# Seven block products for eight in the last feed-forward network of a two-layer trunk, with weight sums by accumulating DMAs

## The chip, the cores and the metric

The kernel runs on one core of one Trainium2 chip. The metric is the time of one execution on the device in microseconds (us), the median over several runs of the same program. The profile is one execution taken by the hardware profiler.

## The reference

256 tokens of width 1024 in float32 go through two layers. Layer 0 is a feed-forward network (FFN), a gMLP mixer and a second FFN; layer 1 is an FFN, a stick-breaking attention on a shared K and V, and a second FFN; a final RMSNorm follows. Each FFN adds half of its result to the residual stream. Its hidden width is 2816. What the change touches is the last FFN and the norm behind it:

```python
def swiglu(h, w_in, w_out):
    gu = h @ w_in                       # [256, 1024] @ [1024, 5632]
    gate, up = jnp.split(gu, 2, axis=-1)
    return (jax.nn.silu(gate) * up) @ w_out   # [256, 2816] @ [2816, 1024]
...
x = x + FFN_RES_SCALE * swiglu(rms_norm(x, ffn_norm[i, 1]), ffn_w_in[i, 1], ffn_w_out[i, 1])
...
return rms_norm(x, final_norm)
```

## The kernel before

All products run on TensorE in float32r. To keep float32 accuracy each operand is split into two float32r parts, high and low, and `mm3` makes three products (low by high, high by low, high by high) for each one of the mathematics. The weights are a stream of pieces of [128, 1024]. `Weights.run_to` loads a piece with a DMA on the SP queue into a buffer `raw`, ScalarE casts it into `whi` (line 81), VectorE subtracts into `wlo` (line 83). There are 7 raw buffers and 9 of each part. A scheduler sets the order of each engine's instructions when the program is built, from the order of the code and from what is ready by its own reckoning; on the chip every engine then runs its list strictly in that order, and an instruction that waits holds up all behind it.

The last FFN works on 11 pairs of 128 hidden features, 256 features in a pair (NPAIR). For pair j, `ffn_in` computes gate and up, each [256 features, 256 tokens], into two PSUM banks (`gd`, `ud`) with 96 products of 256 columns, from 4 pieces of weights. VectorE scales both by 1/rms (lines 449, 451), ScalarE applies silu (450), VectorE multiplies (452), and `split` makes the parts `hhd` and `hld` (153, 154). `out_add` multiplies them with two pieces of the second matrix, tokens on the output's partitions: per pair 2 feature halves by 2 token halves by 2 column halves, 8 block products of [128x128] by [128x512], 24 products of 512 columns on TensorE, summed over all pairs in four banks `yo`. The products into `yo` of pair j stand behind the gate and up of pair j+1, so a whole pair of products covers VectorE's and ScalarE's work on h.

The last three chunks are worked piece by piece, and each piece of the output is added to `xo` (the residual stream, transposed back by `back`), squared and summed on ScalarE, multiplied by the gain on POOL, scaled by 1/rms and stored. POOL's queue has no DMA in this stage before; the only ones issued from it in the whole kernel are four copies within SBUF behind the K and V (line 663).

Of the kernel before, what the change touches and what calls it, by code (L numbers as in the profile page):

```python
# [901 lines left out]
```

## Time and profile before

| what | value |
|---|---|
| median of 3 runs | 1019.25 us (1019.13 to 1019.6) |
| profiled execution, first to last instruction (span) | 1016.9 us |
| mean granted TensorE clock | 0.998 |
| busy: PE, VectorE (DVE), ScalarE (ACT), POOL | 98%, 64%, 49%, 8% of the span |
| bytes from HBM | 176.73 MB, 175 GB/s over the span |
| first product of the last network | at 820.08 us |
| last product of the program | starts at 1009.26 us |

The span leaves out what lies ahead of the first and behind the last instruction; no other time of the profiled execution is given. The median of the runs is 2.35 us above the span. PE is matmul, PEld its weight load. A matmul's duration overlaps the next one's, so the pace is read from the distance of the starts. A row of a group gives busy time and mean duration, then how long the engine idled just ahead of such instructions, and for whom.

### The profile page before, as it was taken

What the parts mean: (1) busy time and instruction counts of PE and PEld (TensorE: products, weight loads), DVE (VectorE), ACT (ScalarE), POOL (GpSimd) and SP (SyncE); (2) the same over time, 40 slices, a digit from 0 to 9 for tenths busy, and PEclk for the clock granted to TensorE, in tenths of its full rate; (3) what the DMA queues carried; (4) which work ended last, traced back from release to release, by engine and by line L of the source; (5) the groups of instructions that cost most, each with busy time, mean ns of one, the idle gap of its engine ahead of it and who ended that gap; (6) DMA issues with size and microseconds to landing.
All of it is one profiled execution on the core that took longest, in us unless ns stands there. A gap on an engine that the chain in (4) does not pass through costs nothing.

```text
span 1016.9 us, 19320 instructions
## 1 busy us (share of the span) xinstructions
PE 998.7 (98%) x8044; PEld 979.4 (96%) x8044; DVE 651.4 (64%) x852; ACT 499.6 (49%) x683; POOL 84.0 (8%) x122
## 2 busy tenths in 40 slices
PE   9999999999999999999999999999998899999997
PEld 8999999999999999999999999999998799999996
DVE  6865665676766774646569655564679975655553
ACT  7543434475544553434348444443476565444433
POOL 3000000010000300000003000000036420000002
PEclk9999999999999999999999999999999999999999
DMA  9965555656545365655564756555642436656511
GB/s 310 325 187 174 185 179 176 187 161 212 186 167 167 125 214 183 187 184 187 180 190 141 239 185 187 182 188 181 193 132 65 137 117 219 188 185 191 183 42 42
DMA packets 135208, 179.56 MB, mean 177 GB/s; under 512 B 5624, under 2 KB 119376, under 8 KB 135120
## 3 DMA queue, kind: packets, MB, share of 16 engines
q1 hardware_dynamic: 134768, 177.76, 54.9%
q8 instruction: 63, 1.03, 0.4%
q0 software_dynamic: 192, 0.52, 0.2%
q14 instruction: 25, 0.20, 0.1%
q10 hardware_dynamic: 160, 0.05, 0.0%
HBM read 176.73 MB, written 1.05 MB: 175 GB/s over the span
## 4 chain that ended last, share of the span: by engine, by line
PE 88%; DVE 6%; issue 2%; ACT 1%; DMA 1%; POOL 1%; SPq 0%; ACTq 0%; POOLq 0%; DVEq 0%
PE yo L148 2%; PE yo L150 2%; PE yo L149 2%; PE gb L148 2%; PE uc L149 2%; PE gc L148 2%; PE ub L149 2%; PE yb L148 2%; PE uc L150 2%; PE ub L150 2%; PE ub L148 2%; PE gb L150 2%; PE uc L148 2%; PE ud L150 2%; PE gc L150 2%
## 5 line engine op out<-in xcount | busy, mean ns | idle before, releaser
L81 ACT CAST whi<-raw 128x1024 fp32r<-128x1024 f32 (+1 forms) x333 | 342.3, 1044 | 403.3 <-issue 219.2
L83 DVE TENSOR_TENSOR wlo<-raw,whi 128x1024 fp32r<-128x1024 f32 (+1 forms) x333 | 400.9, 1221 | 203.2 <-ACT whi L81 202.4
L288 POOL TENSOR_TENSOR acc<-acc,sq 128x256 f32<-128x256 f32 x39 | 33.9, 870 | 566.9 <-ACT sq L287 564.9
L148 PE MATMUL ga<-xnh,wlo 128*128 128x256 f32 x176 | 50.7, 288 | 0.0
L148 PE MATMUL ya<-hha,wlo 128*128 128x256 f32 x176 | 50.0, 284 | 0.1
L148 PE MATMUL yc<-hhc,wlo 128*128 128x256 f32 x176 | 50.0, 284 | 0.1
L148 PE MATMUL yb<-hhb,wlo 128*128 128x256 f32 x176 | 50.0, 284 | 0.0
L148 PE MATMUL gd<-xnh,wlo 128*128 128x256 f32 x176 | 50.0, 284 | 0.0
L148 PE MATMUL gb<-xnh,wlo 128*128 128x256 f32 x176 | 49.9, 283 | 0.0
L148 PE MATMUL gc<-xnh,wlo 128*128 128x256 f32 x176 | 49.9, 283 | 0.0
L149 PE MATMUL ya<-hla,whi 128*128 128x256 f32 x176 | 49.8, 283 | 0.0
L149 PE MATMUL yb<-hlb,whi 128*128 128x256 f32 x176 | 49.8, 283 | 0.0
L149 PE MATMUL yc<-hlc,whi 128*128 128x256 f32 x176 | 49.7, 283 | 0.0
L150 PE MATMUL ud<-xnh,whi 128*128 128x256 f32 x176 | 49.7, 282 | 0.0
L150 PE MATMUL uc<-xnh,whi 128*128 128x256 f32 x176 | 49.6, 282 | 0.0
L149 PE MATMUL ub<-xnl,whi 128*128 128x256 f32 x176 | 49.6, 282 | 0.0
L149 PE MATMUL uc<-xnl,whi 128*128 128x256 f32 x176 | 49.6, 282 | 0.0
L150 PE MATMUL yb<-hhb,whi 128*128 128x256 f32 x176 | 49.6, 283 | 0.0
L148 PE MATMUL ua<-xnh,wlo 128*128 128x256 f32 x176 | 49.6, 282 | 0.0
L150 PE MATMUL ga<-xnh,whi 128*128 128x256 f32 x176 | 49.6, 282 | 0.0
L150 PE MATMUL ub<-xnh,whi 128*128 128x256 f32 x176 | 49.6, 282 | 0.0
L149 PE MATMUL gd<-xnl,whi 128*128 128x256 f32 x176 | 49.5, 281 | 0.0
(286 smaller groups left out, 3367.1 us busy)
## 6 DMA issues: line engine op xcount, KB each, us to landing
raw<-in_ffn_w_in_dram SPq DMA_DIRECT2D x176, 512.0 KB, 4.6
raw<-in_ffn_w_out_dram SPq DMA_DIRECT2D x88, 512.0 KB, 4.2
raw<-in_a_w_in_dram SPq DMA_DIRECT2D x32, 512.0 KB, 4.4
raw<-in_a_w_out_dram SPq DMA_DIRECT2D x16, 512.0 KB, 3.3
raw<-in_b_w_q_dram SPq DMA_DIRECT2D x8, 512.0 KB, 4.4
raw<-in_b_w_o_dram SPq DMA_DIRECT2D x8, 512.0 KB, 4.3
raw<-in_w_kv_dram SPq DMA_DIRECT2D x4, 512.0 KB, 4.2
xin<-in_x_dram SPq DMA_DIRECT2D x4, 256.0 KB, 4.5
```

The source lines that it names most:

```text
L81: ins = nc.scalar.copy(hi[:, cc], raw[:, cc])
L83: ins = nc.vector.tensor_sub(lo[:, cc], raw[:, cc], hi[:, cc].bitcast(F32))
L148: nc.tensor.matmul(o, al, bh, start=first, stop=False, skip_group_check=True)
L149: nc.tensor.matmul(o, ah, bl, start=False, stop=False, skip_group_check=True)
L150: nc.tensor.matmul(o, ah, bh, start=False, stop=last, skip_group_check=True)
L288: nc.gpsimd.tensor_add(acc, acc, s)
```

## The change

In the last FFN the second matrix is multiplied with seven block products per pair instead of eight. The hidden values of a pair form a 2x2 matrix of blocks A (token half by feature half), its weights a 2x2 matrix B (feature half by column half of 512). Four sums of A blocks (S1 to S4) and four sums of B blocks (R1 to R4) enter seven products, one PSUM bank each (`q1` to `q7`); the four output blocks are sums of these banks, formed once at the end on `xo`.

- **A.** `in_half(j, m)` computes gate and up of only 128 features into one bank `i{j}_{m}` (48 products), from the same 4 weight pieces for m = 0 and 1. The bank pool `pi` has one buffer (seven banks are taken by `q`). VectorE scales the whole bank into `gud` (line 905), ScalarE applies silu to half of it (906), VectorE multiplies into `fs` (907). With m = 1 come four additions and subtractions of [128, 128] (910 to 913), a cast of [128, 896] on ScalarE into `fsh` and a subtraction on VectorE into `fsl` (156).
- **B.** The class `Forms` takes the second matrix out of the stream of pieces. `load` brings three blocks of 512 columns into `fraw` (two buffers). `first` splits all three (`fh0`, `fl0`, 1536 wide) and issues an accumulating DMA from POOL that adds the fourth block to two of them. `second` splits these two sums (`fh1`, `fl1`) and issues two more accumulating DMAs, the second of which reads what the first wrote. `third` splits the last two sums (`fh2`, `fl2`). Products 1, 2, 3 need `fl0`, 5 and 7 need `fl1`, 6 and 4 need `fl2`.
- **Buffers.** The stream has 5 raw buffers and 7 of each part, for the whole kernel. In the last FFN all 4 pieces of a pair are held until `in_half(j, 1)` has used them.
- **Order on TensorE.** `in_half(j, 0)`; products 1, 2, 3, 5 of pair j-1; `in_half(j, 1)`; products 7, 6, 4 of pair j-1.

```diff
-RAW_AHEAD = 7
-SPLIT_AHEAD = 5
+RAW_AHEAD = 5
+SPLIT_AHEAD = 4
...
-    rawp = ctx.enter_context(tc.tile_pool(name="rawp", bufs=7))
-    hip = ctx.enter_context(tc.tile_pool(name="hip", bufs=9))
-    lop = ctx.enter_context(tc.tile_pool(name="lop", bufs=9))
+    rawp = ctx.enter_context(tc.tile_pool(name="rawp", bufs=5))
+    hip = ctx.enter_context(tc.tile_pool(name="hip", bufs=7))
+    lop = ctx.enter_context(tc.tile_pool(name="lop", bufs=7))
...
-    plan11 = plan_ffn(1, 1)
+    plan11 = [
+        [[W.add(cols(ffn_w_in[1, 1], c0 + 256 * j, kh)) for c0 in (0, DFF)] for kh in range(2)] for j in range(NPAIR)
+    ]
...
+    psum.close()
+    pools["g"] = ctx.enter_context(tc.tile_pool(name="pi", bufs=1, space=PSUM))
+    pools["y"] = ctx.enter_context(tc.tile_pool(name="pq", bufs=7, space=PSUM))
...
+        def load(self, j):
+            t = fm.tile([P, 3, 512], F32, tag="raw", name=f"fraw{j}")
+            for s, (m, n) in enumerate(((1, 1), (0, 0), (1, 0))):
+                nc.sync.dma_start(t[:, s, :], self.block(j, m, n))
...
+        def split(self, j, step, s0, s1):
...
+                bufs = 1 if step == 2 else 2
+                h = fm.tile([P, n, 512], F32R, tag=f"h{step}", bufs=bufs, name=f"fh{step}_{j}")
+                l = fm.tile([P, n, 512], F32R, tag=f"l{step}", bufs=bufs, name=f"fl{step}_{j}")
+            nc.scalar.copy(h, t[:, s0:s1, :])
+            nc.vector.tensor_sub(l, t[:, s0:s1, :], h.bitcast(F32))
...
+        def first(self, j):
...
+            p["B22"], p["B11"], p["B21"] = self.split(j, 0, 0, 3)
+            nc.gpsimd.dma_start(
+                self.raw[j][:, 0:2, :],
+                self.block(j, 0, 1).unsqueeze(1).broadcast_to([P, 2, 512]),
+                accum_op=ALU.add,
+            )
...
+        def second(self, j):
...
+            p["R3"], p["R1"] = self.split(j, 1, 0, 2)
...
+            nc.gpsimd.dma_start(t[:, 1, :], self.block(j, 1, 1), accum_op=ALU.add)
+            nc.gpsimd.dma_start(t[:, 2, :], t[:, 1, :], accum_op=ALU.add)
...
+        def third(self, j):
...
+            p["R2"], p["R4"] = self.split(j, 2, 1, 3)
...
+        gu = scratch(f"gud{j}_{m}")
+        nc.vector.tensor_mul(pair(gu), pair(bank), bc2(rb))
+        nc.scalar.activation(gu[:, :T], gu[:, :T], AF.Silu)
+        nc.vector.tensor_mul(fs[j][:, 2 * m : 2 * m + 2, :], pair(gu[:, :T]), pair(gu[:, T:]))
+        if m:
...
+            nc.vector.tensor_sub(f[:, 4, :], f[:, 2, :], f[:, 0, :])
+            nc.vector.tensor_add(f[:, 5, :], f[:, 4, :], f[:, 1, :])
+            nc.vector.tensor_sub(f[:, 6, :], f[:, 0, :], f[:, 1, :])
+            nc.vector.tensor_sub(f[:, 7, :], f[:, 3, :], f[:, 5, :])
...
+            split(h, l, f[:, 1:, :])
...
-    for j in range(NPAIR - 2):
-        h = hs.pop(j)
-        for m in range(2):
-            out_add(W.get(plan11["out", j][m], UNIT), chunk(h, m), j == 0 and m == 0, False, range(2))
-        hs[j + 2] = ffn_in("d", j + 2, plan11["in", j + 2])
+    for j in range(1, NPAIR):
+        in_half(j, 0, gbank(f"i{j}_0"))
+        forms.first(j)
+        forms.third(j - 1)
...
+        if j + 1 < NPAIR:
+            forms.load(j + 1)
+        out_add(j - 1, (1, 2, 3, 5))
+        in_half(j, 1, gbank(f"i{j}_1"))
+        forms.second(j)
+        if j + 1 < NPAIR:
+            out_add(j - 1, (7, 6, 4))
+    forms.third(NPAIR - 1)
```

At the end of the program products 7, 6 and 4 of pair 9 and all seven of pair 10 remain; `rest` issues them one by one, and the sums into `xo`, squares and scaling follow each.

**VectorE, last network, a pair in the middle, before.** The rows from the scaling of pair 4's gate and up to the parts of its h and the next weight split (a name's first number is the pair or piece, the last one a running number).

```order
L449 TENSOR_TENSOR gsd_4_10550<-gd_4_10428,rb_119 128x512
L451 TENSOR_TENSOR usd_4_10551<-ud_4_10429,rb_119 128x512
L83 TENSOR_TENSOR wlo299_10601<-raw299_10560,whi299_10600 128x1024
L452 TENSOR_TENSOR usd_4_10551<-usd_4_10551,gsd_4_10550 128x512
L83 TENSOR_TENSOR wlo300_10607<-raw300_10578,whi300_10606 128x1024
L154 TENSOR_TENSOR hld_4_10557<-usd_4_10551,hhd_4_10556 128x512
L83 TENSOR_TENSOR wlo301_10661<-raw301_10598,whi301_10660 128x1024
```

VectorE splits at will between the four steps of h; the products of pair 4 that need `hld_4` stand behind the 96 products of pair 5.

**VectorE, the same place now.** The rows from the scaling of pair 6's second half (`gud6_1`) to that of pair 7's first half (`gud7_0`).

```order
L905 TENSOR_TENSOR gud6_1_11008<-i6_1_10959,rb_119 128x512
L83 TENSOR_TENSOR wlo299_11045<-raw299_11036,whi299_11044 128x1024
L83 TENSOR_TENSOR wlo300_11075<-raw300_11042,whi300_11074 128x1024
L907 TENSOR_TENSOR fs6_10929<-gud6_1_11008 128x256
L844 TENSOR_TENSOR fl1_7_11200<-fraw7_10943,fh1_7_11199 128x1024
L910 TENSOR_TENSOR fs6_10929<-fs6_10929 128x128
L844 TENSOR_TENSOR fl2_6_11119<-fraw6_10764,fh2_6_11118 128x1024
L911 TENSOR_TENSOR fs6_10929<-fs6_10929 128x128
L913 TENSOR_TENSOR fs6_10929<-fs6_10929 128x128
L156 TENSOR_TENSOR fsl6_11017<-fs6_10929,fsh6_11016 128x896
L905 TENSOR_TENSOR gud7_0_11109<-i7_0_11035,rb_119 128x512
```

Between `gud6_1` and `fsl6`, for which products 1, 2, 3 and 5 of pair 6 wait, stand two splits of weight pieces, one split of pair 7's weight sums (`fl1_7`) and one of pair 6's (`fl2_6`).

**ScalarE, the same place now.** The rows between the cast of pair 5's and of pair 6's sums of h (`fsh`).

```order
L906 ACTIVATE gud6_0_10930<-gud6_0_10930 128x256
L843 CAST fh0_7_11113<-fraw7_10943 128x1536
L81 CAST whi297_10901<-raw297_10893 128x1024
L81 CAST whi298_11038<-raw298_10899 128x1024
L81 CAST whi299_11044<-raw299_11036 128x1024
L81 CAST whi300_11074<-raw300_11042 128x1024
L906 ACTIVATE gud6_1_11008<-gud6_1_11008 128x256
L843 CAST fh1_7_11199<-fraw7_10943 128x1024
L843 CAST fh2_6_11118<-fraw6_10764 128x1024
L155 CAST fsh6_11016<-fs6_10929 128x896
```

Four casts of weight pieces stand between the silu of pair 6's two halves; `whi297` to `whi300` take the buffers of the four pieces that `in_half(6, 0)` and `in_half(6, 1)` use, from piece 290 on.

**VectorE, the beginning of the last network now.** The rows of pairs 1 and 2.

```order
L844 TENSOR_TENSOR fl1_1_10126<-fraw1_9859,fh1_1_10125 128x1024
L905 TENSOR_TENSOR gud1_1_10113<-i1_1_10064,rb_119 128x512
L83 TENSOR_TENSOR wlo278_10144<-raw278_9997,whi278_10143 128x1024
L83 TENSOR_TENSOR wlo279_10150<-raw279_10141,whi279_10149 128x1024
L907 TENSOR_TENSOR fs1_10027<-gud1_1_10113 128x256
L83 TENSOR_TENSOR wlo280_10180<-raw280_10147,whi280_10179 128x1024
L910 TENSOR_TENSOR fs1_10027<-fs1_10027 128x128
L844 TENSOR_TENSOR fl0_2_10219<-fraw2_10048,fh0_2_10218 128x1536
L911 TENSOR_TENSOR fs1_10027<-fs1_10027 128x128
L844 TENSOR_TENSOR fl2_1_10224<-fraw1_9859,fh2_1_10223 128x1024
L913 TENSOR_TENSOR fs1_10027<-fs1_10027 128x128
L905 TENSOR_TENSOR gud2_0_10214<-i2_0_10140,rb_119 128x512
```

The sums of pair 1's h (`fs1`) and the scaling `gud2_0`, which frees the only bank for gate and up, stand behind `fl0_2` and `fl2_1`, the latter behind pair 1's three accumulating DMAs.

## Rows read from the trace of the kernel before

**Rows 1.** The page, part 1: busy time, share of the span, instructions.
```profile
PE 998.7 (98%) x8044; PEld 979.4 (96%) x8044; DVE 651.4 (64%) x852; ACT 499.6 (49%) x683; POOL 84.0 (8%) x122
```
**Rows 2.** Stretches: PE, PEld, DVE, ACT, POOL busy; granted clock, DMA share, GB/s.
```profile
745.00:820.00 75.00, 66.81 (x495) 61.82 (x495) 65.96 (x112) 48.38 (x94) 31.07 (x57) 1.00 0.37 119
863.31:880.15 16.84, 16.84 (x122) 15.86 (x121) 9.57 (x11) 7.15 (x9) 0.00 (x0) 1.00 0.59 188
```
**Rows 3.** TensorE in time order around two pairs' ends: start us, us, what.
```profile
863.19 0.28 PE L150 MATMUL ud<-xnh,whi 128*128 128x256 f32 x1
863.31 0.40 PE L148 MATMUL yo<-whi,hld 128*128 128x512 f32 x1
...
864.47 0.40 PE L150 MATMUL yo<-whi,hhd 128*128 128x512 f32 x1
...
880.15 0.40 PE L148 MATMUL yo<-whi,hld 128*128 128x512 f32 x1
```
**Rows 4.** Groups by shape, 840 to 1000 us: busy us, mean ns, idle before, releasers.
```profile
L83 DVE TENSOR_TENSOR wlo<-raw,whi 128x1024 fp32r<-128x1024 f32 x53 | 64.0, 1220 | 41.5 <-ACT whi L81 41.4
L449 DVE TENSOR_TENSOR gsd<-gd,rb 128x512 f32<-128x512 f32 x10 | 6.9, 692 | 30.2 <-PE gd L150 30.2
...
L81 ACT CAST whi<-raw 128x1024 fp32r<-128x1024 f32 x52 | 53.7, 1047 | 76.4 <-issue 43.1 <-PE gd L150 31.4 <-PE yo L150 1.7
L153 ACT CAST hhd<-usd 128x512 fp32r<-128x512 f32 x11 | 6.9, 623 | 5.6 <-DVE usd L452 5.6
```
**Rows 5.** Groups by shape over the whole span: smaller shapes on VectorE and ScalarE.
```profile
L154 DVE TENSOR_TENSOR a1l<-at,a1h 128x256 fp32r<-128x256 f32 x8 | 3.4, 423 | 0.2
...
L320 DVE TENSOR_SCALAR diag<-ident,rT 128x128 f32<-128x128 f32 x12 | 2.9, 284 | 0.3
...
L856 ACT ACTIVATE junk<-xo 128x256 f32<-128x256 f32 x4 | 1.6, 409 | 2.3 <-DVE xo L854 2.3
```
**Rows 6.** VectorE in time order, back to back in the last network.
```profile
931.59 1.23 DVE L83 TENSOR_TENSOR wlo<-raw,whi 128x1024 fp32r<-128x1024 f32 x1
932.73 0.69 DVE L452 TENSOR_TENSOR usd<-usd,gsd 128x512 f32<-128x512 f32 x1
933.34 1.22 DVE L83 TENSOR_TENSOR wlo<-raw,whi 128x1024 fp32r<-128x1024 f32 x1
```
**Rows 7.** ScalarE in time order: casts and what they waited for (in brackets).
```profile
941.40 2.00 ACT L81 CAST whi<-raw 128x1024 fp32r<-128x1024 f32 x2 [3.92 <-PE gd L150]
```
**Rows 8.** The end of the last network in time order.
```profile
997.96 0.28 PE L150 MATMUL ud<-xnh,whi 128*128 128x256 f32 x1
...
1000.46 0.69 DVE L154 TENSOR_TENSOR hld<-usd,hhd 128x512 fp32r<-128x512 f32 x1 [0.69 <-ACT hhd L153]
...
1009.26 0.28 PE L150 MATMUL yo<-whi,hhd 128*128 128x256 f32 x1
```
**Rows 9.** DMA issues: engine, count, KB each, median us from issue to landing.
```profile
raw<-in_ffn_w_in_dram SPq DMA_DIRECT2D x176, 512.0 KB, 4.6
...
xin<-in_x_dram SPq DMA_DIRECT2D x4, 256.0 KB, 4.5
out_dram<-xo SPq DMA_DIRECT2D x4, 256.0 KB, 2.0
...
kzh<-kzh POOLq DMA_DIRECT2D x2, 128.0 KB, 6.2
```
**Rows 10.** The stretch of the POOL queue's copies (columns of rows 2), and their issue.
```profile
554.00:558.00 4.00, 4.00 (x36) 4.00 (x35) 3.94 (x9) 3.20 (x7) 2.51 (x4) 1.00 1.05 347
...
L663 POOL DMA_DIRECT2D kzh<-kzh x2 | 1.4, 684 | 9.2 <-ACT kzh L153 9.2
```
**Rows 11.** The chain of waits in the attention: start us, us, what.
```profile
791.57 2.48 DVE wlo L83 x2
...
798.69 2.59 DVE wlo L83 x2
```
**Rows 12.** The start of the last network in time order, POOL and TensorE.
```profile
821.86 4.25 POOL L288 TENSOR_TENSOR acc<-acc,sq 128x256 f32<-128x256 f32 x5
...
826.81 0.50 PE L311 MATMUL pstf<-ones,acc 128*128 128x1 f32 x4
```

More of the change, by code (lines that the diff above doesn't have):

```diff
@@ L806, in back @@
             for hf in range(2):
-                bank = gbank(f"xb{tt}{hf}")
+                bank = ybank(f"xb{tt}{hf}")
                 for c in range(4):
@@ new lines, in trunk, with out_add @@
+    q = {}
+    def out_add(j, which, last=False, cc=slice(0, 512)):
+        for n in which:
+            a, b = PRODUCTS[n]
+            s = SLOT[a]
+            mm3(
+                q[n][:, cc],
+                tuple(t[:, s, :] for t in fs[j]),
+                tuple(t[:, cc] for t in forms.parts[j][b]),
+                j == 0,
+                last,
+            )
+    norm = Rms("f3")
+    forms.load(0)
+    in_half(0, 0, gbank("i0_0"), (norm.columns, norm.rows))
+    forms.first(0)
+    forms.load(1)
@@ new lines, in trunk @@
+    in_half(0, 1, ybank("i0_1"))
+    back()
+    forms.second(0)
+    for j in range(1, NPAIR):
+        in_half(j, 0, gbank(f"i{j}_0"))
+        forms.first(j)
+        forms.third(j - 1)
+        if j == 1:
+            q = {n: ybank(f"q{n}") for n in range(1, 8)}
+        if j + 1 < NPAIR:
[6 more added lines that the diff above has]
+    forms.third(NPAIR - 1)
@@ new lines, in at, with add, square @@
+    def at(tt, n):
+        return xo[:, tt, n * 512 : (n + 1) * 512]
+    def add(o, a, scale, b):
+        nc.vector.scalar_tensor_tensor(o, a, scale, b, ALU.mult, ALU.add)
+    ss = {tt: small.tile([P, 4], F32, tag="ss", name=f"ss{tt}") for tt in range(2)}
+    def square(tt, i, cc):
+        junk = scratch(f"junk{tt}{i}", cc.stop - cc.start)
+        o = xo[:, tt, cc]
+        nc.scalar.activation(junk, o, AF.Square, accum_out=ss[tt][:, i : i + 1])
+        nc.gpsimd.tensor_mul(o, o, gf[:, cc])
@@ L871, in trunk @@
-        for hf in range(2):
-            cc = slice(hf * 512, (hf + 1) * 512)
-            nc.sync.dma_start(out[tt * P : (tt + 1) * P, cc], xo[:, tt, cc])
+        nc.vector.reduce_sum(v, ss[tt][:, :n], axis=mybir.AxisListType.X)
+        nc.vector.tensor_scalar(v, v, 1.0 / D, RMS_EPS, ALU.mult, ALU.add)
+        nc.scalar.activation(root, v, AF.Sqrt)
+        newton(r[:, 0:1], root, v, r[:, 1:2])
+        nc.vector.tensor_scalar_mul(at(tt, 0), at(tt, 0), r[:, 0:1])
+        nc.scalar.mul(at(tt, 1), at(tt, 1), r[:, 0:1])
@@ new lines, in finish, with rest @@
+        for h in range(2):
+            nc.sync.dma_start(out[tt * P : (tt + 1) * P, h * 512 : (h + 1) * 512], at(tt, h))
+    def rest(n, cc=slice(0, 512)):
+        if n in (7, 6, 4):
+            out_add(NPAIR - 2, (n,), False, cc)
+        out_add(NPAIR - 1, (n,), True, cc)
+    t1 = scratch("t1")
+    t5 = scratch("t5")
+    t6 = scratch("t6")
+    t7 = scratch("t7")
+    rest(1)
+    nc.scalar.mul(t1, q[1], 0.5)
+    rest(6)
+    nc.vector.tensor_add(at(1, 0), at(1, 0), t1)
+    nc.vector.scalar_tensor_tensor(
+        t6, q[6], 0.5, t1, ALU.mult, ALU.subtract
+    )
@@ new lines, in trunk @@
+    rest(5)
+    nc.vector.tensor_add(at(1, 1), at(1, 1), t6)
+    nc.scalar.mul(t5, q[5], 0.5)
+    rest(2)
+    add(at(1, 0), q[2], 0.5, at(1, 0))
+    square(1, 0, slice(0, 512))
+    nc.vector.tensor_sub(at(1, 1), at(1, 1), t5)
+    rest(3)
+    add(at(1, 1), q[3], 0.5, at(1, 1))
+    square(1, 1, slice(512, 1024))
+    rest(7)
+    add(t7, q[7], 0.5, t6)
+    nc.vector.tensor_add(at(0, 1), at(0, 1), t7)
+    nc.vector.tensor_sub(at(0, 1), at(0, 1), t5)
+    square(0, 0, slice(512, 1024))
+    nc.vector.tensor_sub(at(0, 0), at(0, 0), t7)
@@ L876 @@
+    finish(1, 2)
+    for i in range(2):
+        cc = slice(i * 256, (i + 1) * 256)
+        rest(4, cc)
+        add(xo[:, 0, cc], q[4][:, cc], 0.5, xo[:, 0, cc])
+        square(0, 1 + i, cc)
+    finish(0, 3)
 _INS = ['x', 'ffn_norm', 'ffn_w_in', 'ffn_w_out', 'mix_norm', 'a_w_in', 'a_ln_g', 'a_ln_b', 'a_w_s',
```

122 lines of the change are left out of this document (69 added, 53 removed).

## The prediction

> **What bounds the kernel now.** I read the page first: TensorE is busy for 98% of the span, VectorE for 64%, ScalarE for 49% [rows 1]. Then the stretches: in the last network TensorE is busy in all 16.84 us of a pair, VectorE in 9.57 and ScalarE in 7.15; only the attention leaves TensorE idle, 8.2 of its 75 us, with VectorE busy in 66 [rows 2]. TensorE in time order gives its pace: products of 512 columns start 0.232 us apart (five steps from 863.31 to 864.47), a pair takes 16.84 (863.31 to 880.15) [rows 3]. It has 24 of these and 96 of 256 columns, which leaves (16.84 - 24 x 0.232) / 96 = 0.117 for one of the latter. So in the last network the time is the number of products, as long as VectorE and ScalarE deliver in time. The groups show how much air they have: VectorE waits 30.2 us for `gd` and 41.4 for casts, and ScalarE's casts wait for `gd` [rows 4], that is for a weight buffer that TensorE still reads [rows 7].
>
> **What is saved.** One block product of eight, three products of 512 columns per pair: 3 x 0.232 x 11 = **7.65 us**. A pair would take 16.84 - 0.70 = 16.14.
>
> **What VectorE gets.** Durations: 1024 wide 1.22 us, 512 wide 0.69 [rows 4]; 256 wide 0.42, and 0.29 for 128 wide from the nearest shape, a one-input row of 0.284 [rows 5]. Instructions that follow each other start 0.085 sooner than their duration (1.14 and 0.61) [rows 6]. 896 and 1536 wide lie on the line through 512 and 1024: 1.09 and 1.75. Before, a pair has 6 x 1.22 + 4 x 0.69, about 10 us. Now 4 x 1.22 for pieces, 1.75 + 2 x 1.22 for the weight sums, 2 x 0.69 + 2 x 0.42 + 4 x 0.29 + 1.09 for h: 13.5, less 15 x 0.085, or 12.2 of 16.14. That would fit as a sum. It does not fit in its place.
>
> **The list behind each bank.** Count from the end of the last product of gate and up of a pair's second half (pair 6, say). Before, nothing waits soon for h, since 96 products of the next pair come first. Now TensorE has only products 7, 6, 4 of the pair before (9 x 0.232 = 2.09) and the next half (48 x 0.117 = 5.63), and is at product 1 of pair 6 after 7.72 less the overlap of the last product, 0.28 - 0.12: **7.56 us**. Product 1 needs `fsl6`. VectorE's list up to there:
> - Weight splits 297 and 298 stand ahead of `gud6_1` and take buffers that are free only when the first 24 products of this half are done, 24 x 0.117 = 2.81 before its end. Cast 1.05 [rows 4], two subtractions 2.28, two hand-overs 0.1: VectorE is late by 0.6.
> - `gud6_1` 0.61, two splits 2.28, `fs6` 0.34, `fl1_7` 1.14, one sum 0.20, `fl2_6` 1.14, two sums 0.48.
> - The cast of 896 on ScalarE, 0.94 between 0.62 and 1.05 [rows 4], `fsl6` 1.09, hand-overs 0.15.
>
> Together 8.97: TensorE **waits 1.4 us per pair**, twice what it saves. The pair takes 16.14 + 1.4 = 17.5, against 16.84. Nothing on ScalarE ends later: its four casts and the silu fit beside. The bank for gate and up itself is free in time, 1.3 us after the end where TensorE comes back after 2.1. Four sums of [128, 128] more or less in the estimate of 0.29 move this by 0.2 us.
>
> **The accumulating DMAs.** No accumulating DMA is in the trace. Plain neighbours [rows 9]: 256 KB to HBM 2.0 us from issue to landing, 256 KB from HBM 4.5, 512 KB 4.6; the four 128 KB copies from the POOL queue took 6.2, but in a stretch where the DMA engines were busy all the time (share 1.05) [rows 10], where the last network has 0.59 [rows 2]. I take 4.5 for each of the three, the row with the same bytes at the usual load, and keep 2.0 and 6.2 as ends; a gain is excluded, as there was no such wait. POOL is otherwise idle here; each issue costs it 0.68 [rows 10], no more than it has. In the middle of the stage 4.5 is hidden. `fraw` is free after `fl2`, 6.4 after the end above; load 4.5, cast 1.47, `fl0` 1.75 bring the first accumulation to 14.3, and ScalarE reaches `fh1` at 19.9 (17.5 + 2.4): room for 5.6 us. Each us above costs one in every pair. On POOL's queue the third accumulation waits for the second and holds up the next pair's first, which is not due before 14.3, when the third has landed (2 x 4.5 after `fl1` at 5.0). On SP the load of `fraw` waits for `fl2` and holds up the loads of pieces behind it, which have 12 buffers, three pairs, of air.
>
> In pairs 1 and 2 it is not hidden. `gud2_0`, which frees the bank, stands behind `fl2_1`. That needs DMAs two and three of pair 1; these start after `fl1_1`, which stands behind `fl2_0`, which needs DMAs two and three of pair 0. Four in series: 4 x 4.55 = 18.2. Between them: cast 1.05, `fl2_0` 1.14, a split 1.14, `fl1_1` 1.22, cast 1.05, `fl2_1` 1.14, a sum 0.20, `gud2_0` 0.69, hand-overs 0.2: 26.0 us from the end of `fl1_0`. TensorE has 1.0 left of a half there and one pair, 17.2: it waits **8.8 us** in all. Pair 2 still feels it (its `fl0` follows the late `fraw`), by the same lists 2.7.
>
> The Trainium skill (DMA: Bandwidth & Descriptors, Anatomy of one DMA — SWDGE (gpsimd) path) gives about 2.0 us plus the bytes at 436 GB/s, which would be an estimate of 3.2 and 2.6 us here and would bring my sum to about 1027; the copies of rows 10 took 6.2 where that rule gives 2.3, so under load this trace does not agree.
>
> **The ends of the stage.** At the start the one-column products for 1/rms stand behind 35 products, not 48: at 826.8 - 13 x 0.117 = 825.3 the sum of squares, done at 826.1, is not there [rows 12]: 0.8, taken as 1.0 with the hand-over. At the end nothing of the list stands in the way, but h of pair 10 takes 0.69 + 0.41 + 0.42 + 0.77 + 0.94 + 1.09 + 0.2 = 4.5 us (before 2.9, from the end of the last `ud` product at 998.24 to that of `hld` at 1001.15 [rows 8]), and TensorE has only 6 x 0.232 + 3 x 0.117 = 1.74 of other products, where before it had all those of pair 9: it waits **2.9**. Pair 9 waits 0.6 more (its VectorE list is shorter). Behind the last product little changes: the same add, square, root and scaling in two pieces, 0.
>
> **Fewer buffers.** Before the last network TensorE's order is the same. VectorE's chain in the attention has wlo splits in it [rows 11]; with the shorter look-ahead nine instead of ten stand between the first scan and the last values: -1.1, with bounds 0 and -1.2. Elsewhere the stream runs far ahead: 7 pieces cover 7 x 24 x 0.117 = 19.7 us of products, a load and a split take 4.6 + 1.05 + 1.22 = 6.9 [rows 4, 9]. 0.
>
> **The sum.** -7.65 + 1.0 (start) + 8.8 (pairs 0 and 1) + 2.7 (pair 2) + 6 x 1.4 = 8.4 (pairs 3 to 8) + 0.6 + 2.9 (end) - 1.1 = +15.7. The profiled execution's 1016.9 us would become 1032.6; with the 2.35 us by which the median stands above the span, **1035 us**. With 2.0 us for each DMA only the lists are left: pairs 0 to 2 wait 4.1 instead of 11.5 and pair 9 not at all, 1027. With 6.2 pairs 1 and 2 wait 4 x 1.7 = 6.8 and half of that, 3.4, more, pair 0 some 1.5, the end some 4, and six pairs 6.2 - 5.6 = 0.6 each: 19 more, 1054.
>
> **The rivals.**
> - *The list fits, faster.* If VectorE were 1.4 us earlier at `fsl` in each pair (no lateness from splits 297 and 298, and the sums behind each other cheaper than 0.20), and the DMAs took at most 2.5 us, only the start (1.0), pair 0 (1.0) and the end (2.9) would stay: 1019.25 - 7.65 - 1.1 + 4.9 = **1015**. For it: in sum VectorE has 16.1 - 12.2 us of air. Against it: all the durations are rows and the lists are fixed. It decides at a wait of 0.3 us per pair. 12%.
> - *The DMAs are slow, the pairs run at their pace.* From 5.6 us on the first accumulation sets each pair, and the four in series cost 4 us per us: 1054 at 6.2, about 1067 at 7.5. For it: 6.2 us for a quarter of the bytes [rows 10], and an accumulation must also read what it adds to. Against it: the load at that time. 20%. The Trainium skill (SBUF — State Buffer, Who interferes with whom) would push this way, as it says that POOL cannot write a DMA's descriptors while VectorE runs in a two-port mode; the copies of rows 10 were issued in 0.68 us each with VectorE busy in 3.94 of 4 us, so this trace shows no such starving.
> - *A draw.* Waits equal the saving, at 0.3 us per pair and fast DMAs: 1019. 5%.
> - That the change does not do what it says is excluded by the lists: 21 products of 512 columns per pair.
>
> **How the numbers follow.** The forecast has 63%, its own range 1024 to 1050 (DMAs of 2.0 to 5.8 us, the list 0.3 shorter or longer per pair). The range of 8 in 10 goes from 1018 to 1058: it leaves out the fast rival and the upper third of the slow one. A difference of 0.2% is what a measurement here can tell from none. Faster by over 0.2%: 12%. Within: 5%. Slower: 83%.
>
> **What would show it.** The products of a pair, waits aside, take 16.14 us; TensorE waits for VectorE's `fsl` (line 156) about 1.4 us in each of eight pairs, and for `gud2_0` some 6 us around pair 2; VectorE's busy time in a pair is about 13 us; accumulating DMAs land after about 4.5 us; about 3 us idle before product 1 of pair 10. I am wrong if TensorE's waits in the last network stay below 7.65 us, or if `fsl` is done before TensorE comes to it.

## The result and the profile after

The changed kernel takes **1075.43 us** (median of 4 runs, 1074.15 to 1076.56) against 1019.23 before (median of 4): a ratio of 1.055, 95% interval 1.0535 to 1.0565. The forecast was 1035, its range ended at 1058. The profiled execution has a span of 1074.7 us (before 1016.9), so there are 57.8 us to account for.

The page of the changed kernel: its header, then part 1, which answers to [rows 1], and the granted clock in the 40 slices.

```profile
span 1074.7 us, 19465 instructions
...
PE 1006.7 (94%) x7999; PEld 981.8 (91%) x7999; DVE 692.8 (64%) x922; ACT 522.6 (49%) x703; POOL 118.7 (11%) x154
...
PEclk9999999999999999999999999999999988989897
```

TensorE has 45 records fewer and yet 8.0 us more of busy time. Busy time that rises while work falls points to slower work, and the last line says where: the granted clock is below full in five of the last eight slices, which lie in the last network. The groups of waits of TensorE (us in total, times, longest) say what it stood still for:

```profile
PE q L150 <- DVE fsl L156: 27.5, 10, 4.8
PE i L150 <- DVE gud L905: 8.5, 1, 8.5
PE pstx L315 <- POOL acc L292: 5.8, 1, 5.8
PE q L150 <- DVE xo L972: 4.6, 1, 4.6
...
PE pstf L315 <- POOL acc L292: 1.9, 2, 1.6
```

The first, second and last are where the prediction put them. Of the first, 4.2 us belong to pair 0; the other 23.3, in pairs 2 to 10, stand against 14.6 forecast (2.7 + 8.4 + 0.6 + 2.9). The third, at the start of the program, and the fourth, at its end, were in no part of it. TensorE in time order, product 1 of pairs 2 to 10 without pairs 6 and 8, which waited 1.69 and 1.10 us (start us, us; in brackets the idle time before it and what ended it):

```profile
899.32 0.79 PE L150 MATMUL q<-fh,fsl 128*128 128x512 f32 x1 [3.87 <-DVE fsl L156]
...
919.45 0.50 PE L150 MATMUL q<-fh,fsl 128*128 128x512 f32 x1 [0.93 <-DVE fsl L156]
...
940.72 0.79 PE L150 MATMUL q<-fh,fsl 128*128 128x512 f32 x1 [4.81 <-DVE fsl L156]
...
960.66 0.50 PE L150 MATMUL q<-fh,fsl 128*128 128x512 f32 x1 [0.93 <-DVE fsl L156]
...
999.93 0.79 PE L150 MATMUL q<-fh,fsl 128*128 128x512 f32 x1 [4.68 <-DVE fsl L156]
...
1038.17 0.54 PE L150 MATMUL q<-fh,fsl 128*128 128x512 f32 x1 [2.21 <-DVE fsl L156]
...
1053.28 0.80 PE L150 MATMUL q<-fh,fsl 128*128 128x512 f32 x1 [3.11 <-DVE fsl L156]
```

In the middle there are two kinds of wait: some 1 us, near the forecast list wait of 1.4, and 3.9 to 4.8; those of 2.21 and 3.11 are the end's. The second column shows what the waits do to the product behind: 0.50 us behind the short ones, 0.79 behind most of the long ones. Behind the wait of pair 2 all twelve products (1, 2, 3 and 5, three each) ran slowly:

```profile
899.91 0.63 PE L151 MATMUL q<-fl,fsh 128*128 128x512 f32 x1
...
904.18 0.63 PE L152 MATMUL q<-fh,fsh 128*128 128x512 f32 x1
```

These start 0.427 us apart ((904.18 - 899.91) / 10), where products of this shape went at 0.232 before [rows 3]. The windows around them (stretch, length; PE, PEld, DVE, ACT, POOL busy; granted clock, DMA share, GB/s) show the clock: half, 1.2 GHz, and full again at 906:

```profile
902.00:903.00 1.00, 1.00 (x4) 0.76 (x3) 0.00 (x0) 0.00 (x0) 0.00 (x0) 0.50 0.98 178
...
906.00:907.00 1.00, 1.00 (x11) 1.00 (x10) 0.83 (x1) 0.00 (x0) 0.00 (x0) 1.00 0.00 0
```

What the long waits come from stands in the DMA issues of the last network (KB each, median us from issue to landing); the last three rows are the accumulating ones, for which [rows 9] gave the bounds:

```profile
fraw<-in_ffn_w_out_dram SPq DMA_DIRECT2D x33, 256.0 KB, 4.5
fraw<-in_ffn_w_out_dram POOLq DMA_DIRECT2D x11, 512.0 KB, 6.2
fraw<-in_ffn_w_out_dram POOLq DMA_DIRECT2D x11, 256.0 KB, 3.8
fraw<-fraw POOLq DMA_DIRECT2D x11, 256.0 KB, 3.8
```

One of the first kind, followed through POOL, ScalarE and VectorE ahead of product 1 of pair 2 (the three fences are the time orders of these engines):

```profile
886.35 1.20 POOL L850 DMA_DIRECT2D fraw<-in_ffn_w_out_dram  x1 [0.83 <-DVE fl L844]
```
```profile
893.33 2.01 ACT L843 CAST fh<-fraw 128x1024 fp32r<-128x1024 f32 x2 [3.63 <-DMA fraw<-in_ffn_w_out_dram]
```
```profile
894.41 1.23 DVE L844 TENSOR_TENSOR fl<-fraw,fh 128x1024 fp32r<-128x1024 f32 x1 [2.67 <-ACT fh L843]
...
895.75 1.22 DVE L844 TENSOR_TENSOR fl<-fraw,fh 128x1024 fp32r<-128x1024 f32 x1
896.89 0.28 DVE L913 TENSOR_TENSOR fs<-fs 128x128 f32<-128x128 f32 x1
898.17 1.09 DVE L156 TENSOR_TENSOR fsl<-fs,fsh 128x896 fp32r<-128x896 f32 x1 [1.00 <-ACT fsh L155]
```

From the start of the issue to the cast that needs the sum 7.0 us pass. VectorE stands still for 2.67 us at `fl1`, and the last sums of h and `fsl`, which do not need these weights at all, stand behind it in its list. That is the slow-DMA rival at work.

The balance, by parts of the span (forecast from the prediction's sum; measured from starts of the same product in both traces and from TensorE's idle times; the products saved are not measured but counted, at the pace before):

| part | forecast | measured |
|---|---|---|
| program start | 0 | +7.9 |
| pace of the products ahead of the last network | 0 | -3.3 |
| attention | -1.1 | -1.2 |
| products saved (counted) | -7.65 | -7.65 |
| TensorE idle in the last network: start | 1.0 | 1.6 |
| pairs 0 and 1 | 8.8 | 12.7 |
| pair 2 | 2.7 | 3.9 |
| pairs 3 to 8 | 8.4 | 14.1 |
| pair 9 | 0.6 | 2.2 |
| ahead of products of pair 10 | 2.9 | 3.1 + 4.6 |
| products at the lower clock | 0 | +16.5 |
| behind the last product | 0 | +1.0 |
| not assigned | | +2.4 |

The 16.5 are 67 products of 512 columns that start 0.437 us apart on average instead of 0.229, and 23 of 256 at 0.231 instead of 0.118. This is a tally of slow products: time that TensorE would have waited for VectorE even at the full clock is in it too.

### The profile page after: what moved, and what is told of

Its sections match the earlier page's. It is cut to its first block, busy times and chain, and to the rows that moved or that the text cites. A ratio compares the mean times of both kernels' runs of the same rounds, so it can differ in the third digit from the quotient of the medians.

```text
span 1074.7 us, 19465 instructions
## 1 busy us (share of the span) xinstructions
PE 1006.7 (94%) x7999; PEld 981.8 (91%) x7999; DVE 692.8 (64%) x922; ACT 522.6 (49%) x703; POOL 118.7 (11%) x154
## 4 chain that ended last, share of the span: by engine, by line
PE 72%; DMA 9%; DVE 8%; ACT 4%; issue 3%; POOL 2%; SPq 0%; ACTq 0%; POOLq 0%; DVEq 0%
DMA fraw<-in_ffn_w_out_dram 6%; DVE fl L844 2%; PE uc L152 2%; PE uc L151 2%; PE gc L150 2%; PE ua L150 2%; PE gc L151 2%; PE uc L150 2%; PE gc L152 2%; PE ua L151 2%; PE yb L150 2%; PE ua L152 2%; PE yb L152 2%; PE yb L151 2%; PE gb L150 2%
## 5 line engine op out<-in xcount | busy, mean ns | idle before, releaser
L150 PE MATMUL i<-xnh,wlo 128*128 128x256 f32 x352 | 100.2, 285 | 8.5 <-DVE gud L905 8.5
L152 PE MATMUL i<-xnh,whi 128*128 128x256 f32 x352 | 99.7, 283 | 0.0
L151 PE MATMUL i<-xnl,whi 128*128 128x256 f32 x352 | 99.5, 283 | 0.0
L844 DVE TENSOR_TENSOR fl<-fraw,fh 128x1024 fp32r<-128x1024 f32 (+1 forms) x33 | 46.2, 1399 | 60.2 <-ACT fh L843 60.1
L150 PEld LDWEIGHTS i<-xnh,wlo 128*128 128x128 f32 x352 | 67.2, 191 | 9.7 <-DVE gud L905 8.7
L843 ACT CAST fh<-fraw 128x1024 fp32r<-128x1024 f32 (+1 forms) x33 | 38.6, 1190 | 64.4 <-DMA fraw<-in_ffn_w_out_dram 32.8
L151 PEld LDWEIGHTS i<-xnl,whi 128*128 128x128 f32 x352 | 67.2, 191 | 0.8
L152 PEld LDWEIGHTS i<-xnh,whi 128*128 128x128 f32 x352 | 67.1, 190 | 0.0
L151 PE MATMUL ua<-xnl,whi 128*128 128x256 f32 x176 | 50.4, 287 | 0.0
L152 PE MATMUL ua<-xnh,whi 128*128 128x256 f32 x176 | 50.4, 286 | 0.0
```

What stands on the lines that cost most here:

```text
L150: nc.tensor.matmul(o, al, bh, start=first, stop=False, skip_group_check=True)
L151: nc.tensor.matmul(o, ah, bl, start=False, stop=False, skip_group_check=True)
L152: nc.tensor.matmul(o, ah, bh, start=False, stop=last, skip_group_check=True)
L843: nc.scalar.copy(h, t[:, s0:s1, :])
L844: nc.vector.tensor_sub(l, t[:, s0:s1, :], h.bitcast(F32))
```

## The experiments

**The DMAs.** My theory after the result: the accumulating DMAs make the long waits, and the waits the low clock. First the kernel without accumulating DMAs, which leaves the sums of the weights out of the result.

```diff
-            nc.gpsimd.dma_start(
-                self.raw[j][:, 0:2, :],
...
-            t = self.raw[j]
-            nc.gpsimd.dma_start(t[:, 1, :], self.block(j, 1, 1), accum_op=ALU.add)
-            nc.gpsimd.dma_start(t[:, 2, :], t[:, 1, :], accum_op=ALU.add)
```

> The changed kernel without its three accumulating DMAs per pair; all splits stay, so the sums of the second matrix are left out of the computation (R1 to R4 are plain blocks). Theory 'the DMAs set the waits beyond the list': the wait at gud2_0 (8.5 us) goes, the waits for fsl fall to 1.0 to 1.4 us in each pair, the clock stays at 2.4 GHz in the pairs, only the end (3.1 and 4.6 us) remains: idle in the last network 42 -> about 20 us, low clock 17 -> about 6, so about 1042 us. Rival 'VectorE's list is that long by itself': waits for fsl stay at 0.9 to 4.8 us and the time over 1065 us.

Measured: 1038.01 us, ratio 1.0188 (1.0167 to 1.0208). Its waits for `fsl` (`gud` is down to 0.8 us):

```profile
PE q L150 <- DVE fsl L156: 10.9, 9, 3.1
```

Product 1 of two pairs in time order:

```profile
882.13 0.50 PE L150 MATMUL q<-fh,fsl 128*128 128x512 f32 x1 [0.92 <-DVE fsl L156]
899.47 0.50 PE L150 MATMUL q<-fh,fsl 128*128 128x512 f32 x1 [0.92 <-DVE fsl L156]
```

Without these DMAs only the list is left: seven waits of 0.92 us, a pair of 17.34. Products at the lower clock cost some 4.5 us instead of 16.5. The DMAs cost 37 us in all.

Is it the adding, or a DMA as such? The same DMAs that copy instead of adding:

```diff
-                accum_op=ALU.add,
...
-            nc.gpsimd.dma_start(t[:, 1, :], self.block(j, 1, 1), accum_op=ALU.add)
-            nc.gpsimd.dma_start(t[:, 2, :], t[:, 1, :], accum_op=ALU.add)
+            nc.gpsimd.dma_start(t[:, 1, :], self.block(j, 1, 1))
+            nc.gpsimd.dma_start(t[:, 2, :], t[:, 1, :])
```

> The changed kernel with the same three DMAs per pair as plain copies, with no addition (the sums are left out of the computation). Theory 'adding makes the DMA slow': the 512 KB one lands in about 4.5 us where it took 6.2 and the 256 KB ones in about 2.5 where they took 3.8; the waits shrink by about 2 us in every second pair and some 6 us around pair 2, with the clock about 1055 us. Rival 'the queue and the load make it slow, not the addition': 6.2 and 3.8 us stay, the time stays at 1072 to 1077 us.

Measured: 1051.25 us, ratio 1.0318 (1.0297 to 1.0338). The same three rows of its DMA issues:

```profile
fraw<-in_ffn_w_out_dram POOLq DMA_DIRECT2D x11, 512.0 KB, 4.3
fraw<-in_ffn_w_out_dram POOLq DMA_DIRECT2D x11, 256.0 KB, 3.9
fraw<-fraw POOLq DMA_DIRECT2D x11, 256.0 KB, 2.4
```

Adding costs 1.9 us on the first kind and 1.4 on the third, nothing on the second. These 3.3 us per pair are worth 24 us of the time (1075.43 - 1051.25), the copying DMAs that remain 13.

**The clock.** If the lower clock comes from TensorE standing still, useless products in the gaps must bring it back. Sixteen products of 512 columns ahead of product 1, from pair 1 to pair 9:

```diff
+        if j > 1:
+            for _ in range(FILL):
+                nc.tensor.matmul(
+                    q[1], xnh[:, 0, :P], forms.parts[j - 1]["B11"][0], start=False, stop=False, skip_group_check=True
+                )
```

> The changed kernel with 16 extra products of 512 columns ahead of product 1 of each pair from the second on (they are added into q1, so the output has them too much). They need nothing that VectorE makes late, so TensorE works where it waited for fsl. They are 9 x 16 x 0.23 = 33 us of products more. Theory 'the waits lower the clock, and the products behind a long wait pay for it': the waits for fsl behind products of pairs 2 to 10 (23 us) nearly vanish and the clock stays at 2.4 GHz there, 11 us won back: 1075.4 + 33 - 23 - 11 = 1074 us, granted clock above 0.98. Rival 'the clock falls for another reason (what VectorE, ScalarE or the DMAs do)': the stretches at half clock stay, 1085 us or more, granted clock 0.97 or less.

Measured: 1078.08 us, ratio 1.0581 (1.056 to 1.0602). The same stretch of the changed kernel and, second, of this one (columns as in the windows above):

```profile
890.00:910.00 20.00, 16.13 (x102) 14.77 (x101) 9.94 (x15) 6.83 (x7) 2.96 (x3) 0.83 0.75 197
```
```profile
890.00:910.00 20.00, 20.00 (x136) 18.40 (x135) 12.71 (x16) 9.15 (x11) 2.14 (x4) 1.00 0.77 201
```

Nine pairs have 9 x 16 x 0.23 = 33 us more of products, and the time rises by 2.7. What they replace is mostly waiting: TensorE's idle time in the last network falls from 42.2 to 20.8 us, and about half of the 16.5 at the lower clock goes. So the clock follows the gaps, as the theory said, and the rival's 1085 us did not come. From product 1 of pair 2 to that of pair 9 TensorE now works without a pause:

```profile
903.82:1043.17 139.35, 139.35 (x933) 128.16 (x931) 85.59 (x107) 60.76 (x66) 21.60 (x22) 1.00 0.63 164
```

That is 19.91 us for each of seven pairs, which is what TensorE's own products take (16.14 + 16 x 0.23 = 19.8); the changed kernel took 138.85 for the same seven (899.32 to 1038.17). So the DMAs and VectorE's lists keep up with a pair of 19.9 us, but here they do not set it, the useless products do. Fewer of them were not tried, and no run takes away the low clock alone: what it costs by itself stays open.

**The start.** The wait of 5.8 us at `pstx` was not in the prediction. The time orders of POOL at the start of the program, before and, second, after:

```profile
14.11 0.78 POOL L347 TENSOR_TENSOR sqx<-xT 128x256 f32<-128x256 f32 x1 [0.77 <-ACT xT L342]
...
17.43 1.68 POOL L288 TENSOR_TENSOR acc<-acc,sq 128x256 f32<-128x256 f32 x2
25.06 2.07 POOL L500 TENSOR_SCALAR_AFFINE_SELECT wsbs<-wsbs 128x512 f32<-128x512 f32 x2 [5.95 <-DMA wsbs<-in_a_w_s_dram]
```
```profile
17.07 1.23 POOL L504 TENSOR_SCALAR_AFFINE_SELECT wsbs<-wsbs 128x512 f32<-128x512 f32 x2 [3.58 <-DMA wsbs<-in_a_w_s_dram]
18.26 1.58 POOL L351 TENSOR_TENSOR sqx<-xT 128x256 f32<-128x256 f32 x1
...
23.94 1.52 POOL L292 TENSOR_TENSOR acc<-acc,sq 128x256 f32<-128x256 f32 x2
```

The selection on `wsbs`, for which nothing waits early, has moved ahead of the sum of squares, for which TensorE waits, and it waits for its own load first. Theory: the smaller numbers of buffers alone do that. The kernel before, with these alone:

```diff
-RAW_AHEAD = 7
-SPLIT_AHEAD = 5
+RAW_AHEAD = 5
+SPLIT_AHEAD = 4
...
-    rawp = ctx.enter_context(tc.tile_pool(name="rawp", bufs=7))
+    rawp = ctx.enter_context(tc.tile_pool(name="rawp", bufs=5))
```

(`hip` and `lop` likewise, 9 to 7.)

> The kernel before, with nothing but 5 raw buffers and 7 of each part (5 loads and 4 splits ahead). Theory 'POOL at the start': fewer loads ahead let the load of wsbs go out earlier, and with it POOL's selection of wsbs moves ahead of the sum of squares, so that pstx waits some 5.8 us and TensorE's clock falls behind it. The first ya product then comes 7.9 us later than before, and with the 3.3 us won back on the way and 1.2 in the attention the last network begins 3.4 us later: about 1022.7 us. Rival, my prediction's: fewer buffers cost nothing outside the attention and win 1.1 there: 1018.1 us, no wait at pstx.

Measured: 1025.86 us, ratio 1.0073 (1.0056 to 1.009). Its wait:

```profile
PE pstx L311 <- POOL acc L288: 6.0, 1, 6.0
```

The last network begins at 827.05 instead of 820.08. The selection stands ahead of the sum of squares on POOL here too (16.52 against 17.71 us). So "fewer buffers, 0" cost 7 us, by an order on POOL. The expected value was missed by the 3.3 us of pace that this kernel did not gain; where those come from is shown at the pools below. Then the changed kernel with the selection held in its written place:

```diff
-        nc.gpsimd.affine_select(
+        ins = nc.gpsimd.affine_select(
...
+        tc.keep_in_program_order(ins)
```

> The changed kernel with one line more: POOL's selection of wsbs keeps its place behind the sum of squares at the start. Theory 'POOL at the start': the wait at pstx (5.8 us) and the low clock behind it go, 7.9 us in all: 1067.5 us. Rival: the start is late because weight pieces come late with 5 raw buffers; then the wait only moves to the first products of ua and the time stays at 1073 to 1076 us.

Measured: 1072.36 us, ratio 1.0525 (1.0509 to 1.0541). The wait at `pstx` is gone and the last network begins at 816.99, 6.5 earlier, but only 3.1 arrive at the end, between the two values expected: the last network then took 245.25 us from first to last product instead of 242.52. TensorE's idle time in it is the same (42.5 us, before 42.2), only with long waits in other pairs; what grew, by some 2.5 us, is the time at the lower clock. Why a start at another moment changes that was not tried.

**The end.** The changed kernel issues product 4 of pair 10 in two halves, and the second half's bank waits 4.6 us for VectorE's `xo`. In one piece there is no such wait:

```diff
+    rest(4)
...
-        rest(4, cc)
```

> The changed kernel with one thing else at its end: product 4 of pairs 9 and 10 is made in one piece of 512 columns, so that it doesn't wait for VectorE to read the first half of q4. Theory 'VectorE's list sets the end': TensorE's wait of 4.6 us for xo goes, but the end gains 1.3 us only, since VectorE comes to q4 at 1064.8 either way: 1074.1 us. Rival 'the wait is on the path': 1070.8 us.

Measured: 1076.21 us, ratio 1.0554 (1.0539 to 1.0569): no difference. The wait is gone from its list of waits and the end stays, so it was off the path: VectorE's sums set the end. Without the wait 14.9 us lie behind TensorE's last product, where 7.7 lay in the kernel before. In them one row stands out, here of the changed kernel (VectorE, and POOL beside it):

```profile
1060.81 0.68 DVE L972 SCALAR_TENSOR_TENSOR t<-q,t 128x512 f32<-128x512 f32 x1
...
1061.81 1.78 DVE L1023 TENSOR_TENSOR xo<-xo,t 128x512 f32<-128x512 f32 x1
1063.52 0.68 DVE L1026 TENSOR_TENSOR xo<-xo,t 128x512 f32<-128x512 f32 x1
```
```profile
1060.46 2.58 POOL L980 TENSOR_TENSOR xo<-xo,gf 128x512 f32<-128x512 f32 x2 [21.62 <-ACT junk L979]
```

While POOL multiplies, an addition of two SBUF tiles takes 1.78 us, and one that reads a bank takes 0.68 as ever. The Trainium skill (SBUF — State Buffer, Who interferes with whom) says just this of VectorE instructions outside its two-port modes: one with two SBUF inputs contends with a POOL instruction that reads SBUF, one with a single SBUF input does not. The trace agrees.

**The pools.** The changed kernel's products ahead of the last network start 0.1182 us apart, those of before 0.1188. The change also opens its pools in another order, so the tiles lie elsewhere. Theory: the addresses alone do it. The kernel before, with `small` opened ahead of `scr` and `hp` and nothing else changed:

```diff
-    hp = ctx.enter_context(tc.tile_pool(name="hp", bufs=4))
-    scr = ctx.enter_context(tc.tile_pool(name="scr", bufs=8))
...
+    scr = ctx.enter_context(tc.tile_pool(name="scr", bufs=8))
+    hp = ctx.enter_context(tc.tile_pool(name="hp", bufs=4))
```

> The kernel before with three lines exchanged: the pool 'small' is opened ahead of the pools 'scr' and 'hp', as the change does, so that these tiles lie at other addresses; the order of instructions is the same on every engine. In the changed kernel the products ahead of the last network start 0.1182 us apart where before it is 0.1188, 3.3 us over the networks. Theory 'addresses': the pace becomes 0.1182 here too: about 1015.5 us. Rival 'something else in the change': 1019 us as before.

Measured: **1016.26 us**, ratio 0.9976 (0.9965 to 0.9986), the best version of all. The last network begins at 816.52 instead of 820.08. The same stretch of TensorE's products, before and, second, here:

```profile
40.00:200.00 160.00, 160.00 (x1335) 158.72 (x1335) 96.48 (x116) 66.33 (x76) 0.00 (x0) 1.00 0.61 191
```
```profile
40.00:200.00 160.00, 160.00 (x1344) 158.71 (x1343) 97.01 (x119) 66.63 (x77) 0.00 (x0) 1.00 0.60 191
```

TensorE is busy throughout at the full clock in both, with nine products more in 160 us. From the same first product at 35.50 it reaches the attention's first at 735.91 instead of 739.43: 0.5% in the pace, 0.1188 to 0.1182. That it is the place of tiles is shown. The trace also narrows down which: only products that read h (from the pool `hp`, one of the three moved) change, from 0.1197 to 0.1178 us, while those that read `xnh` and `xnl` take 0.1182 in both. In the last network the products of h with 512 columns go the other way, from 0.229 to 0.234, which gives 1.1 us back there (190.29 from first to last product, before 189.18). What in TensorE's way it is stays open.

**Can seven products win?** Four versions tried to keep the saving. All have the changed kernel's pools, so the 3.3 us of pace are in them too and are not the seven products' doing. The first gives each step half a pair more: products 1, 2, 3, 5 of pair j-1 behind both halves of pair j, products 7, 6, 4 behind the first half of pair j+1, the weight sums held in their written order.

```diff
+        if j > 1:
+            out_add(j - 2, (7, 6, 4))
...
-        in_half(j, 1, gbank(f"i{j}_1"))
-        forms.second(j)
-        if j + 1 < NPAIR:
-            out_add(j - 1, (7, 6, 4))
```

> The changed kernel with each pair's seven products half a pair later (1, 2, 3, 5 of pair j-1 behind both halves of pair j, 7, 6, 4 behind the first half of pair j+1), so that 13 to 16 us of products cover h instead of 7.6; the splits of the weight sums pinned behind the halves; POOL's selection at the start pinned; at the end q4 read in one piece and q6 behind q7. Still three accumulating DMAs per pair. Theory 'list and DMAs are the whole loss, the clock follows': no wait for fsl; but fl2 stands 4 us behind gud0 and its DMAs land 9.4 us behind fl1, so that gud1 comes up to 1.8 us late in each pair: 1012 us without that, 1030 with it. Rival 'the seven products lose for another reason': over 1040 us.

Measured: 1056.1 us, ratio 1.0366 (1.0345 to 1.0386), a clear miss. Its waits:

```profile
PE i L150 <- DVE gud L907: 20.4, 14, 2.7
PE q L150 <- DVE fsl L156: 3.6, 1, 3.6
```

The waits for `fsl` are gone but for one; now `gud`, which frees the bank, stands behind `fl2`, which waits for the DMAs (VectorE idles 3.6 us at it per pair). The wait has moved to another row of the same list. So the second version takes the DMAs away, all but the first: block 11 is loaded a second time and VectorE makes the two other sums.

```diff
-            nc.gpsimd.dma_start(t[:, 1, :], self.block(j, 1, 1), accum_op=ALU.add)
-            nc.gpsimd.dma_start(t[:, 2, :], t[:, 1, :], accum_op=ALU.add)
+            tc.keep_in_program_order(nc.vector.tensor_add(t[:, 1, :], t[:, 1, :], t[:, 2, :]))
+            tc.keep_in_program_order(nc.vector.tensor_add(t[:, 0, :], t[:, 0, :], t[:, 1, :]))
```

> As b1_late, with one accumulating DMA per pair instead of three: B11 is loaded twice, the DMA makes R1 and R3, VectorE makes R2 and R4 with two additions of [128, 512] (2 x 0.61 us); gf takes a raw buffer at the end. VectorE then has 13.4 of a pair's 16.1 us. Theory: nothing waits in the pairs: last network begins at 817.0, 181.5 us of products at full clock, 1.6 us at its start, 1 at the end, 7.6 behind the last product, 2 between span and time: 1011 us, faster than both. Rival 'VectorE is too full, a wait of 1 us in each pair comes back': 1021 us.

Measured: 1026.56 us, ratio 1.0073 (1.0058 to 1.0088): 30 us back, but above both values expected. `gud` waits 4.4 us in four places, `fsl` 2.6 once. A wait of 1.57 us at the start of the network, which the changed kernel has too, is here followed by 3.4 us at half the clock, where there none was (the second line is a window):

```profile
824.26 0.61 PE L315 MATMUL pstf<-ones,acc 128*128 128x1 f32 x4 [1.57 <-POOL acc L292]
...
825.81:829.22 3.41, 3.41 (x18) 3.41 (x18) 2.33 (x8) 0.68 (x2) 0.00 (x0) 0.50 0.99 345
```

The last product is at 1012.22, the span ends at 1025.3: 13.1 behind it, before 7.6. The third version rearranges the end: products of pair 10 in the order 1, 3, 6, 2, 5, 7, 4, and the last pair's weight sums made earlier.

```diff
-    rest(5)
+    rest(3)
+    add(at(1, 1), q[3], 0.5, at(1, 1))
...
+    rest(6)
```

> As b2_adds, with the last pair's weight sums ready earlier (its fl0 ahead of fl1 of pair 9, its additions and fl1 ahead of its second half, fl2 between fsh and fsl), the products of pair 10 in the order 1, 3, 6, 2, 5, 7, 4, and the table for the square root loaded ahead of them. In b2_adds gud0_10 came 1.1 us late, product 1 of pair 10 waited 2.6 us and 2.7 more went to the half clock behind it, and 13 us lie behind the last product. Theory 'what is left in b2_adds is its end': the waits and the half clock at pair 10 go (6 us), and 2 to 4 us of the 13 behind the last product: 1016 to 1019 us. Rival 'the last pair's DMA is late whatever the order': the waits come back at fl1 of pair 10, 1023 us or more.

Measured: 1027.31 us, ratio 1.0079 (1.0066 to 1.0091), no gain, as the rival said: the last pair's `gud` came 2.8 us late, and POOL's multiplications stretched VectorE's additions again, to 1.43 and 1.41 us where alone they take 0.68. The fourth takes POOL out of the end and gives the last pair's blocks stream buffers, so that they load early.

```diff
-        nc.gpsimd.tensor_mul(o, o, gf[:, cc])
...
+            nc.vector.scalar_tensor_tensor(at(tt, h), at(tt, h), r[:, 0:1], gf[:, cc], ALU.mult, ALU.mult)
```

> As b3_end, with the last pair's blocks of the second matrix loaded into two buffers of the stream of pieces (they are free by then), so that the load doesn't wait for fl2 of pair 8 and fl0 of pair 10 comes 2 to 4 us earlier; and with no work on POOL at the end: gain and 1/rms are one instruction of VectorE (in b3_end VectorE's additions within SBUF took 1.4 us in place of 0.7 where POOL multiplied by the gain). Theory 'b3_end lost at gud0_10 (2.8 us of waiting and about 2.9 of half clock behind it) and to POOL at the end (some 3 us)': 1018 us. Rival 'the end takes 13 us because VectorE has eleven additions there, POOL or not': 1021 us or more.

Measured: 1021.21 us, ratio 1.002 (1.0011 to 1.0029); the rival was right. TensorE's last product and VectorE's last sum in time order:

```profile
1006.27 0.40 PE L152 MATMUL q<-fh,fsh 128*128 128x512 f32 x1
```
```profile
1010.33 0.69 DVE L1066 SCALAR_TENSOR_TENSOR xo<-q,xo 128x512 f32<-128x512 f32 x1
```

TensorE is done 3.0 us earlier than before (1009.26 [rows 8]), but these are not the products' saving: the network begins 3.3 us earlier (816.81 instead of 820.08), and the same begin is had with eight products (816.52 in the run with the exchanged pools, which at 1016.26 us beats this version by 5). From first to last product the network takes 189.46 us, before 189.18. In the middle the saving is there, six pairs of 16.22 us each where one took 16.84 [rows 3]:

```profile
899.25:996.57 97.32, 97.32 (x704) 91.60 (x703) 82.06 (x108) 51.15 (x58) 7.21 (x6) 1.00 0.68 194
```

Waits of 5.1 us in all, at the start and in pairs 2 and 3, and a stretch at half the clock behind the first of them eat most of it. Behind the last product the sums of seven banks end only at 1011.0, the scaling at 1016.0 and the span at 1019.4: 13.1 us, 7.6 before.

## Why the prediction was wrong

The direction, the place of the waits and their releasers were right, the size was not: 16 us forecast, 56 measured. The run with copying DMAs divides the 40 us between forecast and measurement. Its DMAs land after 4.3, 3.9 and 2.4 us, near the 4.5 assumed, and it takes 1051.25: 24 us of the miss come with the time that adding takes (1075.43 - 1051.25), the other 16 (1051.25 - 1035) with terms that the sum put at nothing. In that run the waits themselves were not too low: TensorE stands still for 20.9 us of the last network besides the wait for `xo`, where 24.4 were forecast (1.0 + 8.8 + 2.7 + 8.4 + 0.6 + 2.9). Above the sum are some 9 us of products at the lower clock, a later begin of the network (822.58 instead of 820.08 - 1.1) and 5.6 us at the end.

- **"The list behind each bank: 1.4 us."** Right, a little high: 0.92 where no DMA disturbs it, pair 17.34 where 17.5 was forecast. The durations read off the line (1.75 and 1.09) and from the nearest shape (0.29) hold: 1.76, 1.09 and 0.28.
- **"I take 4.5 for each of the three."** This step failed first, and cost most. The first accumulation lands after 6.2 us, and the upper end of the range was the right value for it; the other two took 3.8. The neighbours were plain loads; a plain copy in the same place takes 4.3, so the row was right for a copy and not for an addition. POOL's issues take 1.20, 0.90 and 0.86 us, not 0.68 [rows 10]. The case was priced as the slow-DMA rival, 1054 at 6.2 us, with 20%.
- **"Each us above costs one in every pair."** Only nearly. The pairs have long and short waits in turn, 14.1 us in pairs 3 to 8 instead of the rival's 8.4 + 6 x 0.6 = 12.0.
- **A wait is worth its length.** Nowhere written and everywhere used. Behind the long waits TensorE's products ran at 1.2 GHz, 16.5 us by the tally of the balance; with copying DMAs some 9, without these DMAs some 4.5. How much of it the end of the program feels was not separated.
- **"Fewer buffers ... elsewhere 0."** Wrong: 7.9 us lost by POOL's order at the start. The argument was that TensorE's order is the same there, which it is; POOL's is not. Another 3.3 us came back from the pace, by addresses, which the sum did not have either.
- **The end.** 2.9 forecast, 3.1 measured ahead of product 1 of pair 10; the wait of 4.6 behind it was missed. It is off the path, but only because VectorE's sums of the seven banks end late either way: "behind the last product 0" was wrong by the 4.6 and the 1.0 together.
- **Attention, start.** -1.1 forecast, -1.2 measured; 1.0 forecast, 1.6 measured.

The rival's 1054, with 16.5 for the clock, 3.4 for the later begin of the last network (+7.9 - 3.3 - 1.2) and the 1.1 that the sum had credited to the attention, makes 1075. That these parts add up so well is partly luck: 2.4 us are not assigned, and the end holds errors of both signs.

## What to carry to other kernels

When a change puts TensorE behind a short list, price each wait twice: its length, and the products behind it at half pace. A run with useless products in the gaps shows whether the clock follows the gaps; try fewer and more of them, because they can set the pace themselves. An engine's list is in order, so one late DMA delays all that stands behind it, needed or not: find the DMA's consumer in the list and count what follows. When buffer numbers change, compare the order on every engine over the whole program, also where the edit is far away. When pools move, compare with a kernel whose tiles have moved likewise: here the place of tiles is worth 2.7 us.

## What was not expected of the hardware

- In the changed kernel no product ran at the lower clock behind waits of 0.93 to 1.69 us; behind those of 2.2 us and longer some did, and behind 3.87 us twelve products of 512 columns in a row. Filled with products, the same stretch kept a granted clock of 1.00. The length of the wait alone does not decide it: in the first of the four later versions none ran slowly behind a wait of 2.64 us, in the second 3.4 us went at half the clock behind one of 1.57.
- An accumulating DMA of 512 KB from HBM took 6.2 us (a copy 4.3; adding in the other runs 5.5 to 7.3 by their medians), one of 256 KB from HBM 3.8 (3.9), one of 256 KB inside SBUF 3.8 (2.4).
- Tiles at other addresses alone changed the pace of the products of 256 columns that read h from 0.1197 to 0.1178 us, and that of those with 512 columns from 0.229 to 0.234: together 2.7 us of this kernel.
